# Adding loads of three units, later silu and closer first loads in a one-core decoder layer

## The chip, the core and the metric

The kernel runs on one core of one Trainium2 chip. The metric is the device time of one launch in microseconds, lower being better. One core has five engines with a queue of instructions each: TensorE (PE; PEld is its loading of weights), VectorE (DVE), ScalarE (ACT), GpSimd (POOL) and SyncE (SP). SP only issues transfers (DMA), and POOL issues some too. Each engine works through its queue in order, and an instruction that waits holds everything behind it on the same engine.

## The reference

A decoder layer over 256 tokens of width 2048 in float32, with three blocks, each added to the stream:

- `x + 1/2 * SwiGLU_1(rms(x))`, where `SwiGLU(h) = (silu(h @ w_gate) * (h @ w_up)) @ w_down` with an inner width of 5632,
- a mixer: one projection `h @ w_in` to q, k, v, u, v_sg and two gates; dilated causal attention in three groups beside a gated spatial mixing; both projected, weighted by sigmoid gates, summed and projected by `w_out`,
- `x + 1/2 * SwiGLU_2(rms(x))`, then a final RMS norm.

Nearly all of the work is products of 256 x K activations with weights that are read from memory (the page counts 466 MB read in all).

## The kernel before

**Products.** A float32 product is made of three products of rounded halves: the weights are split into `wh` (a rounded copy, made by ScalarE) and `wl = w - wh` (by VectorE), the activations into `xhi`, `xlo` likewise. A product of 512 columns over one weight tile of 128 x 512 is `xhi*wh + xhi*wl + xlo*wh` for each of the two blocks of 128 tokens.

**Steps and units.** An ordinary step takes two weight tiles (a raw unit of 512 KB, loaded by SP into one of four rooms, asked for four units ahead), has ScalarE and VectorE split them into a ring of nine places (`split`, lines 376 to 390), and issues 12 matmuls. This is one unit of the planner's time. `split` runs four steps ahead of the matmuls; a place of the ring is free when the matmuls of the step four back are done.

**Quads.** Two products that stand beside each other (gate and up, or two column blocks) share part of their K range by the seven-product scheme of Strassen and Winograd. Such a stretch is a quad. It has four blocks of weights, `b11`, `b21` (from the first product) and `b12`, `b22` (from the second), which the code numbers 0, 1, 2, 3, and `nq` units in each. Seven forms (p1 to p7) are split and multiplied in half-unit steps of 6 matmuls (for `nq` = 4: two steps of two units' tiles for each form). Three of the forms are sums that VectorE makes first: `f = b12 + b22`, `t2 = f - b11`, `t1 = t2 - b22` (written over `b11`), `t4 = b21 - t2`. t2 and t4 lie in the tile V. Forms of the activations are sums too (`sums_of`, lines 461 to 484: four small operations on VectorE, then a copy on ScalarE and a difference on VectorE).

In each product pair of the SwiGLU halves (`nq` = 4, 8 ordinary steps) the order is n p5 n p4 n p3 n p2, then p1 of the next quad, n n, p6 of the next, n, p7 of the next, n. So a quad's p1, p6, p7 come at the end of the pair before it, and its p5, p4, p3, p2 in its own pair. One pair takes 15 units.

**Rooms and loads of blocks.** All quads of a home (a SwiGLU half, or the mixer's `gates` and `merge`) use the same four rooms. `move_in` (line 308) asks for the blocks of a home's first quad at set waits. After that, `split` asks for a block of the next quad once the form that read the room last has been split: p5 frees block 0, p2 block 1, p7 block 2, p3 block 3 (`FREES`), 1 unit later for p5 and 2 units later for the others (line 390). Blocks are 1 MB at `nq` = 4.

**The adding load.** In the homes of the SwiGLU halves, all quads but the first let the DMA make f: after the load of block 2 (by SP), POOL issues loads of block 3's weights that add onto block 2's room (`accum_op`, lines 326 to 329), two units at a time: two loads of 512 KB at `nq` = 4, one of 512 KB and one of 256 KB at `nq` = 3, one of 512 KB at `nq` = 2. Block 3 itself is loaded too, for t1 and p3. 17 quads with adding loads have `nq` = 4 (8 in the first half, 9 in the second), four have 3, eight have 2.

**When the sums are made.** `prepare_ready` (line 347) runs after each step. It makes the next sum of a quad's list when its blocks were asked for 3 units ago, its forms are split and VectorE's metered load allows it; or, without those conditions, when the first step that needs it is within two steps of being split. At `nq` = 4 this second case holds for t2 in all 17 quads: it is emitted right behind the split of p1. A unit or more before it, SP was asked for block 3.

**Silu and hold.** When the up product of an inner block f closes, `post_up` runs `go` (silu of the gate on ScalarE), a unit later `mul` (VectorE), then a `turn` (`blocks`: VectorE transposes, SP writes 512 KB to memory; `back`, 3 units later: SP reads it in four loads of 128 KB; `ev`, 8 units later: the split into hA, hB). At some f the turned tile also gives sums for the down product's quads (f=0 and 1 in the first part of each half, f=4, f=8). Those still read the tile that the next silu writes. `holds["sg"]` keeps the next `post_up` back, a unit at a time, until `let_go`, which `sums` calls as `then()` right after its four operations.

**Extras.** `extra` puts VectorE work on a heap with a due time; `work_off` emits it when the metered load allows, at the latest when due.

Of the kernel before, what the change touches and what calls it, by code (L numbers as in the profile page):

```python
# [14 lines left out]
OP = mybir.AluOpType  # L15
# [33 lines left out]
FULL = 2.9  # L49
# [22 lines left out]
def layer(ctx: ExitStack, tc: tile.TileContext, a, out):  # L72
# [41 lines left out]
    x = big.tile([P, NT, D], F32, name="x")  # L114
# [33 lines left out]
    def lay_out():  # L148
        i, count = 0, 0
        while i < len(gemms):  # L150
            g = gemms[i]
            size, stage = g["group"]
            quad = g["quad"]
            taken = range(quad["k0"] // 2, quad["k0"] // 2 + quad["nq"]) if quad else ()
            order = [(p, q) for p in range(size) for q in range(gemms[i + p]["nk"] // 2) if q not in taken]
            if stage:
                order.sort(key=lambda s: stage(*s, gemms[i + s[0]]["nk"] // 2))
            new = [("n", (gemms[i + p], q // 2, q % 2)) for p, q in order]
            if quad:
                nq = quad["nq"]  # L160
                quad["gemms"] = gemms[i], gemms[i + 1]
                quad["loaded"], quad["split"] = {}, set()
                quad["adds"] = quad["home"] in homes and any(q["home"] is quad["home"] for q in quads)
                quad["todo"] = ["t2", "t1", "t4"] if quad["adds"] else ["f", "t2", "t1", "t4"]
                chunks = [(0, nq)] if nq < 4 else [(q, q + 2) for q in range(0, nq, 2)]
                for k, form in opening(count):
                    for c in chunks:
                        steps.insert(len(steps) - k, ("s", (quad, form, *c)))
                for k, form in reversed(list(closing(len(order)))):
                    for c in reversed(chunks):  # L170
                        new.insert(k, ("s", (quad, form, *c)))
                quads.append(quad)
                for h in quad["gemms"]:
                    h["left"] = [3 * (h["nk"] - nq)] * NT
                gemms[i + 1]["left"][1] += 9 * nq
            steps.extend(new)
            count = len(order) if size > 1 else 16
            i += size
        t, pos = -1.0, 0
        for kind, s in steps:  # L180
            width = 2 if kind == "n" else s[3] - s[2]
            t += 1 if kind == "n" else width / 4
            ends.append(t)
            slots.append([(pos + q) % RING for q in range(width)])
            pos += width
            if kind == "s":
                s[0].setdefault("at", {}).setdefault(s[1], len(ends) - 1)
            if kind == "n":
                hus.append(s)
                s[0]["steps"] += 1  # L190
            else:
                s[0]["gemms"][s[1] in ("p3", "p5", "p6", "p7", "p1")]["steps"] += 1
# [21 lines left out]
    def at(i, fn):  # L214
        heapq.heappush(callbacks, (i, next(counter), fn))

    now = [0.0, 0.0]
# [90 lines left out]
    def move_in(home):  # L308
        home["room"] = home["make"](home)
        first = next(q for q in quads if q["home"] is home)  # L310
        for b, wait in ((0, 0), (2, 1.5), (3, 3), (1, 5)):
            at(now[0] + wait, lambda b=b: load_block(first, b))

    def block(quad, b):
        g, j, nq = quad["gemms"][b // 2], b % 2, quad["nq"]
# [3 lines left out]
    def load_block(quad, b):  # L319
        if quad is None:  # L320
            return
        if not quad["loaded"]:
            started.append(quad)
        quad["loaded"][b] = now[0]
        SP.dma_start(blocks_of(quad)[b], block(quad, b))
        if b == 2 and quad["adds"]:
            for q in range(0, quad["nq"], 2):
                c = slice(q, min(q + 2, quad["nq"]))
                POOL.dma_start(blocks_of(quad)[b][:, c], block(quad, 3)[:, c], accum_op=OP.add)  # L329

    def blocks_of(quad):
        r = quad["home"]["room"]
        return [v[:, 0:quad["nq"]] for v in r[:-1]] + [r[-1]]

    def prepare(quad, what):
        b11, b21, b12, b22, t2, t1, _ = blocks_of(quad)
        out, x, y, op = {"f": (b12, b12, b22, OP.add), "t1": (t1, t2, b22, OP.subtract),
                         "t2": (t2, b12, b11, OP.subtract), "t4": (t2, b21, t2, OP.subtract)}[what]
        DVE.tensor_tensor(out, x, y, op=op)

# [6 lines left out]
    def prepare_ready():  # L347
        for quad in started:
            if not quad["todo"]:
                continue  # L350
            what = quad["todo"][0]
            blocks, forms = NEEDS[what]
            urgent = quad["at"]["p6" if what == "f" else next(f for f in USES if USES[f] == what)] - done <= 2
            if (all(quad["loaded"].get(b, 1e9) + (0 if urgent else 3) <= now[0] for b in blocks)
                    and quad["split"].issuperset(forms)
                    and (urgent or DVE.load + 0.56 * quad["nq"] <= FULL)):
                prepare_next(quad)

    def prepare_for(quad, form):
# [16 lines left out]
    def split(i, k=None):  # L376
        kind, s = steps[i]
        if kind == "s":
            quad, form, q0, q1 = s
            prepare_for(quad, form)  # L380
            if q1 == quad["nq"]:
                quad["split"].add(form)
        r = raws[place[i]] if kind == "n" else form_of(quad, form)[:, q0:q1]
        for first, end in runs(i, k or range(len(slots[i]))):
            o = slots[i][first]
            wh, wl = (v[:, o:o + end - first] for v in ring)
            ACT.activation(wh, r[:, first:end], AF.Copy)  # L387
            DVE.tensor_tensor(wl, r[:, first:end], wh.bitcast(F32), op=OP.subtract)
        if kind == "s" and form in FREES and q1 == quad["nq"]:
            at(now[0] + (1 if form == "p5" else 2), lambda: load_block(next_of(quad), FREES[form]))  # L390

    def product(g, t, act, w):
        g["left"][t] -= 1
# [67 lines left out]
    def sums_of(i, keep, q0, nq, store, v, name, tag="gate", slack=1, then=None):  # L461

        got = {}

        def sums():
            w = v[:, 0:4 * nq].rearrange("p (q m) i b -> p m q i b", m=4)
            a0, a1, b0, b1 = (w[:, m] for m in range(4))
            shape = [P, 4, nq, P]
            got["f"] = f = tmp(shape, f"fs{name}") if tag == "tmp" else sb.tile(shape, F32, tag=tag, bufs=2, name=f"fs{name}")
            s1, s2, s3, s4 = (f[:, k].rearrange("p q (i b) -> p q i b", b=32) for k in range(4))  # L470
            DVE.tensor_tensor(s1, a1, b1, op=OP.subtract)
            DVE.tensor_tensor(s2, a0, s1, op=OP.subtract)
            DVE.tensor_tensor(s3, a1, a0, op=OP.subtract)
            DVE.tensor_tensor(s4, b0, s2, op=OP.subtract)
            if then:
                then()
            at(now[0] + min(2, slack), parts)

        def parts():
            keep["both"] = both = store()  # L480
            split_psum(*both, got["f"], slack // 2)
            keep.setdefault("forms", {}).update({q0 + q: [v[:, :, q] for v in both] for q in range(nq)})

        at(i + 1, lambda: extra(0, slack, 0.6 + 0.6 * nq, sums) if slack > 1 else sums())
# [63 lines left out]
    xT = {}  # L548
# [58 lines left out]
    def turn_x(i, n, c, lag, read=3):  # L607
        def evac(src):
            for k in range(4 * c, 4 * c + 4):
                v, g = src[:, 2 * (k - 4 * c):2 * (k - 4 * c) + 2], gcols[:, 16 * n + k:16 * n + k + 1]  # L610
                ACT.activation(v, v, AF.Copy, scale=g)  # L611
            hi, lo = (turned(xT[p][:, 4 * c:4 * c + 4]) for p in ("hi", "lo"))
            split_psum(hi, lo, src, 1 if n and c < 3 else 0)
            tag = "tmp"
            if c == CS[n]:
                sums_of(i + lag, xT, 0, 2, forms_tile(big, "oT", f"fx{n}", 2), src, f"x{n}", tag)
            elif n != 1 and c == CS[n] + 1:
                def store():
                    return [big.tile([P, 4, 2, P], F32R, tag=tag, name=f"fy{n}{tag}") for tag in ("k2", "spare")]

                sums_of(i + lag, xT, 2, 2, store, src, f"y{n}", tag)

        turn(i, f"x{n}_{c}", 8, put_tokens(lambda: x[:, :, c * NC:(c + 1) * NC]),
             lambda: flat(sb.tile([P, NT, NC], F32, tag="gate", bufs=2, name=f"xt{n}_{c}")), evac, lag, read)
# [747 lines left out]
```

## Time and profile before

| | us |
|---|---|
| median of 3 runs | 2032.39 |
| lowest, highest | 2026.04, 2035.64 |
| the profiled execution | 2033.3 |
| its span, first to last instruction | 2031.6 |
| busy in the span: PE | 1981.2 |
| PEld | 1719.4 |
| DVE | 1660.8 |
| ACT | 1231.9 |
| POOL | 76.8 |
| mean granted clock of PE | 0.991 |

The time of an execution is the span plus 1.7 us around it. Busy times of different engines overlap. PE's matmuls are pipelined, and a busy PE is shown with modelled ends, so the number of matmuls in a stretch says more than its busy time. A line number in a row (L66, L329) is that of the kernel; L66 is the helper through which all VectorE operations go, so rows of VectorE are told apart by the tiles they write and read (`V<-quads` is t2, `quads<-V,quads` is t1, `wl<-raw,wh` is the split of an ordinary step). In a row `[7.04 <-DMA quads<-...]` the engine stood idle for 7.04 us before the instruction, and a transfer ended that. SPq and POOLq mark rows of the queues that issue transfers.

### The profile page before, as it was taken

How to read it: one execution, taken by the hardware profiler on the slowest of the kernel's cores; microseconds unless marked ns; L12 is line 12 of the kernel's file. 1: busy time of each engine (PE TensorE's matmuls, PEld its weight loads, DVE VectorE, ACT ScalarE, POOL GpSimd, SP SyncE). 2: the span in 40 equal slices, each digit the busy share in tenths (PEclk: the TensorE clock that was granted, in tenths of full speed). 3: DMA queues.
4: the chain of work that ended last, by engine and by line, in shares of the span. 5: the costliest groups of instructions: out<-in, count | busy, mean ns of one | idle time of the engine just before them, and what ended most of it. 6: DMA issues, size and time to landing. Idle time of an engine off the chain costs nothing.

```text
span 2031.6 us, 25234 instructions
## 1 busy us (share of the span) xinstructions
PE 1981.2 (98%) x9131; PEld 1719.4 (85%) x9131; DVE 1660.8 (82%) x1745; ACT 1231.9 (61%) x1472; POOL 76.8 (4%) x69
## 2 busy tenths in 40 slices
PE   9999999998999989999999999999999999999998
PEld 8788888887888878888888888888888888878887
DVE  6799898987998679676665777899998899888886
ACT  6466566665666566454554555676665566656664
POOL 0000010000000000000000000000000000000000
PEclk9999999999999999999999999999999999999999
DMA  9788878787877885888778667788779778877783
GB/s 302 264 253 243 282 223 274 240 269 210 268 223 230 257 298 171 245 277 267 256 236 256 207 208 227 233 261 273 249 244 272 229 238 252 252 223 245 231 269 134
DMA packets 266821, 497.32 MB, mean 245 GB/s; under 512 B 17228, under 2 KB 45768, under 8 KB 266568
## 3 DMA queue, kind: packets, MB, share of 16 engines
q1 hardware_dynamic: 253288, 470.01, 70.2%
q0 software_dynamic: 13088, 25.17, 7.4%
q8 instruction: 71, 1.16, 0.2%
q10 hardware_dynamic: 320, 0.53, 0.1%
q14 instruction: 54, 0.44, 0.1%
HBM read 465.99 MB, written 29.66 MB: 244 GB/s over the span
## 4 chain that ended last, share of the span: by engine, by line
PE 62%; DVE 8%; DMA 6%; issue 5%; ACT 1%; POOL 0%; SPq 0%; DVEq 0%; POOLq 0%; ACTq 0%
PE qd L394 43%; PE mm L394 18%; DVE wl L66 5%; DMA quads<-in_ffn_w_up_dram 3%; DMA raw<-in_w_in_dram 1%; ACT wh L387 1%; DMA quads<-in_w_in_dram 1%; DVE V L66 1%; DMA xt<-bmx 1%; DMA bmh529.0_10447<-bth529.0_10444 0%; DVE quads L66 0%; ACT xt L611 0%; POOL quads L329 0%; DVE xlo L66 0%; DVE btx L66 0%
## 5 line engine op out<-in xcount | busy, mean ns | idle before, releaser
L66 DVE TENSOR_TENSOR wl<-raw,wh 128x1024 fp32r<-128x1024 f32 (+1 forms) x593 | 647.0, 1110 | 205.1 <-ACT wh L387 202.7
L387 ACT ACTIVATE wh<-raw 128x1024 fp32r<-128x1024 f32 (+1 forms) x593 | 567.5, 966 | 362.2 <-PE qd L394 187.8
L387 ACT ACTIVATE wh<-quads 128x1024 fp32r<-128x1024 f32 (+2 forms) x315 | 308.3, 987 | 229.0 <-PE qd L394 206.5
L394 PE MATMUL qd<-wl,xhi 128*128 128x512 f32 x1106 | 420.9, 381 | 12.3 <-DVE wl L66 12.3
L394 PE MATMUL qd<-wh,xhi 128*128 128x512 f32 x1106 | 419.9, 380 | 1.9 <-ACT wh L387 1.9
L394 PE MATMUL qd<-wh,xlo 128*128 128x512 f32 x1106 | 419.3, 379 | 0.6 <-DVE xlo L66 0.6
L66 DVE TENSOR_TENSOR wl<-quads,wh 128x1024 fp32r<-128x1024 f32 (+2 forms) x315 | 349.7, 1136 | 76.6 <-ACT wh L387 74.8
L394 PEld LDWEIGHTS qd<-wl,xhi 128*128 128x128 f32 x1106 | 209.0, 189 | 47.7 <-DVE wl L66 18.4
L394 PE MATMUL mm<-wl,xhi 128*128 128x512 f32 x608 | 231.2, 383 | 7.8 <-DVE wl L66 7.8
L394 PEld LDWEIGHTS qd<-wh,xhi 128*128 128x128 f32 x1106 | 209.0, 189 | 33.9 <-ACT wh L387 4.2
L394 PE MATMUL mm<-wh,xlo 128*128 128x512 f32 x608 | 233.0, 383 | 1.7 <-DVE xlo L66 1.7
L394 PEld LDWEIGHTS qd<-wh,xlo 128*128 128x128 f32 x1106 | 209.0, 189 | 30.2 <-DVE xlo L66 1.0
L394 PE MATMUL mm<-wh,xhi 128*128 128x512 f32 x608 | 233.1, 383 | 0.0
L394 PE MATMUL qd<-wl,hA 128*128 128x512 f32 x564 | 217.0, 385 | 13.2 <-DVE wl L66 13.2
L394 PE MATMUL qd<-wh,hB 128*128 128x512 f32 x564 | 216.6, 384 | 0.0
L394 PE MATMUL qd<-wh,hA 128*128 128x512 f32 x564 | 216.3, 384 | 0.0
L387 ACT ACTIVATE wh<-V 128x1024 fp32r<-128x1024 f32 (+2 forms) x128 | 124.6, 995 | 93.0 <-PE qd L394 46.2
L66 DVE TENSOR_TENSOR wl<-V,wh 128x1024 fp32r<-128x1024 f32 (+2 forms) x128 | 143.0, 1141 | 16.1 <-ACT wh L387 15.2
L394 PEld LDWEIGHTS mm<-wl,xhi 128*128 128x128 f32 x608 | 116.1, 191 | 26.1 <-DVE wl L66 9.6
L394 PEld LDWEIGHTS qd<-wl,hA 128*128 128x128 f32 x564 | 108.3, 192 | 30.2 <-DVE wl L66 14.4
L394 PEld LDWEIGHTS mm<-wh,xlo 128*128 128x128 f32 x608 | 116.2, 191 | 19.0 <-DVE xlo L66 2.4
L394 PEld LDWEIGHTS mm<-wh,xhi 128*128 128x128 f32 x608 | 116.1, 191 | 16.9 <-ACT wh L387 0.4
(435 smaller groups left out, 2398.6 us busy)
## 6 DMA issues: line engine op xcount, KB each, us to landing
raw<-in_w_in_dram SPq DMA_DIRECT2D x168, 512.0 KB, 4.9
raw<-in_ffn_w_down_dram SPq DMA_DIRECT2D x120, 512.0 KB, 5.2
raw<-in_ffn_w_gate_dram SPq DMA_DIRECT2D x92, 512.0 KB, 4.2
raw<-in_ffn_w_up_dram SPq DMA_DIRECT2D x92, 512.0 KB, 5.8
quads<-in_ffn_w_gate_dram SPq DMA_DIRECT2D x38, 1024.0 KB, 7.9
quads<-in_ffn_w_up_dram SPq DMA_DIRECT2D x38, 1024.0 KB, 7.8
quads<-in_ffn_w_up_dram POOLq DMA_DIRECT2D x34, 512.0 KB, 8.1
quads<-in_ffn_w_down_dram SPq DMA_DIRECT2D x32, 512.0 KB, 5.2
```

The lines of the kernel that those rows point to most:

```text
L66: return method(out, *args, **kwargs)
L387: ACT.activation(wh, r[:, first:end], AF.Copy)
L394: PE.matmul(g["ps"][t], act, in_turn(w), start=not g["begun"][t], stop=g["left"][t] == 0, skip_group_check=g["quad"] is not None)
```

## The change

Four things are changed.

- The adding load takes up to three units in one DMA. At `nq` = 4 the fourth unit's f is made by VectorE (`f` on the slice from 3 to 4), which puts "f" ahead of t2 in those quads' lists, and with it the need for block 3.
- The load of block 2 (and with it the adding load) is asked for 1 unit after the split of p7 in place of 2.
- `let_go` after `sums` comes 2 units after the sums. The activation sums of the second column block before the second half (`y2`) become extra work with a slack of 3 units; until now they were made at once, one unit after the column block.
- `move_in` asks for the blocks 0, 2, 3, 1 at 0, 1, 2 and 3.5 units in the SwiGLU halves in place of 0, 1.5, 3 and 5, and all at once for `gates` and `merge`.

```diff
@@ lay_out
-                quad["todo"] = ["t2", "t1", "t4"] if quad["adds"] else ["f", "t2", "t1", "t4"]
+                quad["added"] = min(nq, 3) if quad["adds"] else 0
+                quad["todo"] = ["f"] * (quad["added"] < nq) + ["t2", "t1", "t4"]
@@ move_in
-        for b, wait in ((0, 0), (2, 1.5), (3, 3), (1, 5)):
-            at(now[0] + wait, lambda b=b: load_block(first, b))
+        late = home in homes
+        for b, wait in ((0, 0), (2, 1), (3, 2), (1, 3.5)):
+            at(now[0] + wait * late, lambda b=b: load_block(first, b))
@@ load_block
         if b == 2 and quad["adds"]:
-            for q in range(0, quad["nq"], 2):
-                c = slice(q, min(q + 2, quad["nq"]))
-                POOL.dma_start(blocks_of(quad)[b][:, c], block(quad, 3)[:, c], accum_op=OP.add)
+            c = slice(0, quad["added"])
+            POOL.dma_start(blocks_of(quad)[b][:, c], block(quad, 3)[:, c], accum_op=OP.add)
@@ prepare
-        out, x, y, op = {"f": (b12, b12, b22, OP.add), "t1": (t1, t2, b22, OP.subtract),
+        if what == "f":
+            c = slice(quad["added"], quad["nq"])
+            DVE.tensor_tensor(b12[:, c], b12[:, c], b22[:, c], op=OP.add)
+            return
+        out, x, y, op = {"t1": (t1, t2, b22, OP.subtract),
                          "t2": (t2, b12, b11, OP.subtract), "t4": (t2, b21, t2, OP.subtract)}[what]
@@ prepare_ready
-                    and (urgent or DVE.load + 0.56 * quad["nq"] <= FULL)):
+                    and (urgent or DVE.load + 0.56 * (quad["nq"] - (what == "f") * quad["added"]) <= FULL)):
@@ split
-            at(now[0] + (1 if form == "p5" else 2), lambda: load_block(next_of(quad), FREES[form]))
+            at(now[0] + (2 if form in ("p2", "p3") else 1), lambda: load_block(next_of(quad), FREES[form]))
@@ sums_of, sums
             if then:
-                then()
+                at(now[0] + 2, then)
@@ turn_x
-                sums_of(i + lag, xT, 2, 2, store, src, f"y{n}", tag)
+                sums_of(i + lag, xT, 2, 2, store, src, f"y{n}", tag, slack=3 if n else 1)
```

## The prediction

> **What bounds the kernel now.** I read the page first, then TensorE's gaps one by one, then the windows around them, then the DMA queues behind those windows.
>
> ```profile
> PE 1981.2 (98%) x9131; PEld 1719.4 (85%) x9131; DVE 1660.8 (82%) x1745; ACT 1231.9 (61%) x1472; POOL 76.8 (4%) x69
> ```
>
> TensorE bounds the kernel, and nothing in the change touches a matmul. So only time that TensorE loses can move. The windows view of the stretches where it loses most (columns: width, busy us and instructions of PE, PEld, DVE, ACT, POOL, then granted clock, DMA share, GB/s):
>
> ```profile
> 240.00:280.00 40.00, 40.00 (x187) 35.03 (x186) 37.38 (x35) 24.27 (x27) 8.48 (x6) 1.00 0.79 245
> 465.00:480.00 15.00, 9.47 (x33) 7.63 (x32) 8.23 (x8) 5.02 (x6) 0.00 (x0) 0.79 0.65 187
> 1575.00:1590.00 15.00, 11.95 (x48) 9.86 (x47) 10.64 (x9) 6.92 (x8) 0.00 (x0) 0.89 0.55 170
> 1800.00:1815.00 15.00, 10.36 (x37) 8.31 (x36) 8.86 (x10) 5.42 (x7) 0.00 (x0) 0.78 0.67 199
> 325.00:332.00 7.00, 5.96 (x28) 4.89 (x28) 6.22 (x5) 4.68 (x6) 0.00 (x0) 1.00 1.05 379
> 1845.00:1855.00 10.00, 8.20 (x38) 6.86 (x38) 6.60 (x7) 5.37 (x7) 0.00 (x0) 1.00 0.73 210
> 1888.00:1895.00 7.00, 6.25 (x30) 5.15 (x29) 5.39 (x5) 4.73 (x6) 0.00 (x0) 1.00 1.06 345
> 348.00:358.00 10.00, 8.16 (x36) 6.28 (x35) 7.72 (x11) 9.05 (x11) 2.31 (x2) 1.00 0.90 226
> 1913.00:1923.00 10.00, 8.20 (x36) 6.32 (x35) 8.62 (x11) 8.18 (x10) 0.00 (x0) 1.00 0.62 162
> 78.00:98.00 20.00, 16.43 (x61) 13.27 (x60) 18.65 (x18) 8.95 (x11) 0.00 (x0) 0.83 0.54 168
> 715.00:735.00 20.00, 14.77 (x56) 11.89 (x55) 15.01 (x15) 11.16 (x16) 0.00 (x0) 0.83 0.75 260
> 1350.00:1356.00 6.00, 3.81 (x18) 2.69 (x16) 6.00 (x7) 5.97 (x10) 0.00 (x0) 1.00 0.62 183
> ```
>
> The first row is a full stretch: 187 matmuls in 40 us, 0.214 us each, so a unit (12 matmuls) is 2.57 us. Where the clock stayed at 1.00, the loss is width minus PE busy. Where it fell, I count missing matmuls instead: 15 us hold 70, so the rows at 465, 1575 and 1800 miss 37, 22 and 33, or 7.9, 4.7 and 7.1 us.
>
> **The change part by part. First the adding load.** The first six short windows (465 to 1888) have one cause. t2 (V<-quads on VectorE) waits for the second adding load, and that one is issued only when the first has landed:
>
> ```profile
> L66 DVE TENSOR_TENSOR V<-quads 128x2048 f32<-128x2048 f32 (+2 forms) x36 | 66.3, 1842 | 25.5 <-DMA quads<-in_ffn_w_up_dram 21.8 <-issue 3.6
> ```
> ```profile
> 453.64 1.22 POOL L329 DMA_DIRECT2D quads<-in_ffn_w_up_dram  x1 [31.61 <-DVE hB L66]
> 462.18 1.21 POOL L329 DMA_DIRECT2D quads<-in_ffn_w_up_dram  x1 [7.32 <-issue]
> ```
> ```profile
> 463.51 1.23 DVE L66 TENSOR_TENSOR wl<-quads,wh 128x1024 fp32r<-128x1024 f32 x1 [0.72 <-ACT wh L387]
> 471.77 2.29 DVE L66 TENSOR_TENSOR V<-quads 128x2048 f32<-128x2048 f32 x1 [7.04 <-DMA quads<-in_ffn_w_up_dram]
> ```
> ```profile
> quads<-in_ffn_w_up_dram POOLq DMA_DIRECT2D x34, 512.0 KB, 8.1
> ```
> ```profile
> quads<-in_ffn_w_down_dram POOLq DMA_DIRECT2D x4, 256.0 KB, 11.7
> ```
>
> Two halves in a row take 8.1 + 8.1 = 16.2 us. In the four quads of three units the 512 KB and 256 KB loads go out together, and the later half lands 11.7 us after its issue; I take 12 us for one load of 768 KB. That is 4 us sooner, and the raw block's load moves one step ahead (half a unit, 1.3 us; it passes at most one raw load of 512 KB, asked for four units ahead). The six waits of VectorE behind the TensorE losses are 1.6 to 7.0 us. 5.3 us clears all but at most 1.7 us of the longest, about the cover that is worked out below. Taken off: 7.9 + 4.7 + 7.1 + 1.04 + 1.80 + 0.75 = **23.3 us**. At the low end (one load of 768 KB as slow as two halves) only 1.3 us at each of six, 7.8 us.
>
> **What the fourth unit costs.** The 17 quads of four units outside the first get an f of 128x512 on VectorE ahead of t2:
>
> ```profile
> L66 DVE TENSOR_TENSOR V<-V,qd 128x512 f32<-128x512 f32 x36 | 24.5, 679 | 0.0
> ```
>
> That is 0.68 us each, 11.5 us in all, and no bound by itself: VectorE is idle 2.6 of 40 us in the full stretch above. What matters is the wait that f brings. It reads block 3, of which until now only t1 had need, some three units later. By the planner's due times f stands where t2 stood, and block 3 is asked for 0.5 to 1.5 units ahead of it. Behind a waiting f on VectorE stand the wl of the next unit, t2, and the wl after it. How long may f wait?
>
> ```profile
> 512.53 2.29 DVE L66 TENSOR_TENSOR V<-quads 128x2048 f32<-128x2048 f32 x1
> 514.73 1.22 DVE L66 TENSOR_TENSOR wl<-raw,wh 128x1024 fp32r<-128x1024 f32 x1
> ```
> ```profile
> 516.79 0.38 PE L394 MATMUL qd<-wl,xhi 128*128 128x512 f32 x1
> ```
>
> Now the next wl ends at 515.95 and is used at 516.79: 0.8 us of cover. With the new order (f 0.68, wl 1.14, t2 2.20, wl 1.22, from 512.53) the second wl ends at 517.8 and is used a unit later, at 519.4: 1.6 us of cover. So TensorE loses what f waits beyond 1.6 us. The first and the last of the 17 quads, in the order asked, landed after so many us, t2:
>
> ```profile
> 122.06 0.49 SPq L325 DMA_DIRECT2D quads<-in_ffn_w_up_dram  x1
> ```
> ```profile
> quads<-in_ffn_w_up_dram SPq DMA_DIRECT2D x1, 1024.0 KB, 6.6
> ```
> ```profile
> 127.28 2.28 DVE L66 TENSOR_TENSOR V<-quads 128x2048 f32<-128x2048 f32 x1
> ```
> ```profile
> 1881.51 2.31 SPq L519 DMA_DIRECT2D sg680.5_13320<-bmh687.5_13361  x4
> 1883.92 0.85 SPq L283 DMA_DIRECT2D raw<-in_ffn_w_up_dram  x1
> 1884.81 0.74 SPq L325 DMA_DIRECT2D quads<-in_ffn_w_up_dram  x1
> ```
> ```profile
> quads<-in_ffn_w_up_dram SPq DMA_DIRECT2D x1, 1024.0 KB, 9.8
> ```
> ```profile
> 1880.73 1.21 POOL L329 DMA_DIRECT2D quads<-in_ffn_w_up_dram  x1 [7.10 <-DVE wl L66]
> ```
> ```profile
> 1889.65 2.29 DVE L66 TENSOR_TENSOR V<-quads 128x2048 f32<-128x2048 f32 x1 [1.61 <-DMA quads<-in_ffn_w_up_dram]
> ```
>
> In the first, block 3 lands at 128.7 against t2's 127.3: f would wait 1.4 us. In the last it lands at 1894.6, and t2 could have begun at 1888.0: 6.6 us. Here SyncE stood at the read-back of the turned h (L519) until 1881.5, and the second adding load shared the DMA engines. All 17 worked out this way wait 59 us, 35 of it beyond 1.6. But the second adding load goes away, and alone block 3 took 6.6 us. With 6.9 us, a little over that, nine quads whose block 3 is asked for without a read-back ahead wait under 1.6 us; three more join them since the silu edit moves their read-back behind block 3. The other five (f=4 and 8 of both halves, f=0 of the second) wait 4.2, 3.1, 3.4, 3.1 and 3.7 us: 17.5 - 5 x 1.6 = 9.5 us lost. I add 3.5 for landings that scatter: **+13 us**, between 0 and 35.
>
> **Silu two steps back.** At five places like the windows at 348 and 1913 (the first and the last of five) ScalarE stands in a silu whose tile VectorE is still reading for sums:
>
> ```profile
> 348.37 1.27 ACT L655 ACTIVATE sg117.5_2540<-qd,rstd 128x512 f32<-128x512 f32 x2 [5.17 <-DVE fsh109.5_2523 L66]
> ```
>
> TensorE loses 1.8 us in each of the two windows, some 8 us over the five. The sums are emitted at their last due time there, so two steps later means that the whole tail of that f (silu, product, two transposes, a write of 512 KB and four reads of 128 KB on SP's queue) comes one unit later, while ScalarE goes on with the wh that wait behind it. New cost: the sums' copy and the silu now stand together on ScalarE (2.3 us), and in the first half the shift passes on from f=1 to f=3, whose h the down product needs at once. I take **-6 us**; bounds -8 and 0.
>
> **The openings.** Each first quad asks for its blocks closer together: in the windows at 78 and 715 TensorE loses 32 and 37 matmuls, 7.0 and 8.0 us.
>
> ```profile
> 73.60 1.22 DVE L66 TENSOR_TENSOR wl<-raw,wh 128x1024 fp32r<-128x1024 f32 x1 [2.65 <-ACT wh L387]
> 74.75 2.28 DVE L66 TENSOR_TENSOR quads<-quads 128x2048 f32<-128x2048 f32 x1
> ```
> ```profile
> 720.21 1.22 DVE L66 TENSOR_TENSOR quads<-quads 128x1024 f32<-128x1024 f32 x1 [4.92 <-DMA quads<-in_w_in_dram]
> ```
>
> At 74.75 the first f comes a unit sooner, into the 2.65 us in which VectorE stood idle: -3 us (0 to -7). At 720, block 3 passes three raw loads and one of 768 KB on SP's queue and lands some 3 us sooner, but those raw loads then go behind 1.5 MB more and hold the next wh: -1.5 us (+5 to -5). In the third opening block 1 goes ahead of the read-back of x (its due time, 3.5 after the start, precedes that of the read-back):
>
> ```profile
> 1366.23 2.84 SPq L519 DMA_DIRECT2D xt<-bmx  x4
> 1369.34 0.39 SPq L283 DMA_DIRECT2D raw<-in_ffn_w_gate_dram  x1
> 1370.84 0.39 SPq L325 DMA_DIRECT2D quads<-in_ffn_w_gate_dram  x1
> ```
>
> 1 MB more ahead at the 260 GB/s of the row at 715 is 4 us; I take it that what follows the read-back has no cover: +4 us (0 to +6). The y2 sums with slack 3 leave the crowded stretch at 1350 (2.2 us lost): -2 us (+2 to -2). Together **-2.5 us**. The four loads of merge come at once too: 0, since none of the losing windows lies there, or +2 if raw loads fall behind.
>
> **Sum:** -23.3 + 13 - 6 - 2.5 = -18.8 us. The profiled execution took 2033.3 us (0.9 above the median, so no correction): 2033.3 - 18.8 = **2014.5 us**.
>
> **The rivals.** (1) *Block 3 becomes the wait.* If its landings stay as they are, f loses 35 us instead of 13, and seven of the 17 losses are 3.0 us or longer, where the clock falls: the windows at 465, 1575 and 1800 lost 2 to 3 us beyond their idle time. At 2 us each that is 14 more: 2033.3 - 23.3 + 49 - 8.5 = 2050, slower. It decides once the 17 waits beyond 1.6 us exceed 32 us with their clock. For it: the last quad above; against it: the load that shared its time goes. The Trainium skill (TensorE: Matmul & The Clock Gate, Part 1: The HAM clock gate) has the clock fall only after an idle window of about 3.4 us; the window at 1575 fell to 0.89 after a shorter gap (12.0 busy of 15), so the row is used. By the page four of the seven would pay: 2044. (2) *One load of 768 KB lands as late as two.* Then t2 keeps waiting: -7.8, f waits beside it (+9.5 at the five quads), silu -6, openings -2.5: about 2026. For it: 11.7 us for 256 KB beside 512 KB; against it: that is still under 16.2. (3) *The gains are given back at the openings:* the bursts push raw loads, +5 at the mixer, +6 in the third, +2 for y2 and nothing at the first, and silu brings 0: 2033.3 - 23.3 + 13 + 13 = 2036, or with silu's 6 about 2030. (4) *Block 3 never decides* and all windows close: 2033.3 - 23.3 - 8 - 7 = 1995.
>
> **How the numbers follow.** Forecast 0.48 (its own range 2004 to 2023), rival 1 0.13, rival 2 0.09, rival 3 0.17, rival 4 0.13. Some 0.5% (10 us) is what a measurement of this kernel can tell from no change: faster is below 2022, slower above 2042.5. Faster: nearly all of the forecast, rival 4, a little of 2: 0.62. Slower: rival 1 and a corner of 3: 0.14. Same: 0.24. The range of 1996 to 2042 leaves out rival 1 and the far half of rival 4.
>
> **What would show it.** One POOL row per quad at the adding line, none released by the one before; t2's idle time on the adding load near 0 (now 21.8); a new row of VectorE, quads<-quads 128x512 x17, with idle time on quads<-in_ffn_w_up_dram: under 20 us by the forecast, 59 by rival 1. Silu without the 5 us idle rows. The windows at 465, 1575 and 1800 back at clock 1.00. Wrong would be a t2 or f that still waits over 3 us in more than two quads, or raw loads late after 720 and 1370.

## The result and the profile after

The changed kernel takes **2044.74 us** (median of 4 runs, 2043.85 to 2048.88) beside 2030.26 us for the kernel before on the same chip. The ratio is **1.0074, 95% interval 1.0044 to 1.0103**: about 15 us slower, where 18.8 us faster was forecast. The profiled execution took 2048.88 us, its span is 2047.2.

The page after, engines and the adding loads (last figure: median us from issue to landing):

```profile
PE 1981.4 (97%) x9131; PEld 1711.0 (84%) x9131; DVE 1670.7 (82%) x1762; ACT 1226.1 (60%) x1472; POOL 53.7 (3%) x48
...
quads<-in_ffn_w_up_dram POOLq DMA_DIRECT2D x17, 768.0 KB, 9.6
```

TensorE's work is the same, 9131 matmuls. VectorE has 17 instructions and 10 us more. The load of 768 KB lands 9.6 us after its issue (12 was taken). The groups of instructions by shape, after; the first is t2, the second f:

```profile
L66 DVE TENSOR_TENSOR V<-quads 128x2048 f32<-128x2048 f32 x19 | 43.4, 2284 | 0.0
...
L66 DVE TENSOR_TENSOR quads<-quads 128x512 f32<-128x512 f32 x17 | 11.7, 690 | 35.0 <-DMA quads<-in_ffn_w_up_dram 31.7 <-DMA gcols<-gm 3.4
```

t2's 21.8 us of idle time on the adding load are gone. f's wait has come in its place: VectorE stands idle 35.0 us ahead of the 17 f. What TensorE waited for, before and then after (total us, times, longest):

```profile
PE qd L394 <- DVE wl L66: 27.2, 22, 5.5
...
PE qd L394 <- DVE V L66: 1.7, 2, 1.6
```
```profile
PE qd L399 <- DVE wl L66: 28.3, 40, 2.6
PE qd L399 <- DVE V L66: 10.2, 11, 1.7
PE qd L399 <- DVE hB L66: 6.2, 2, 3.5
```

The waits for wl are about as long in total as before, in 40 pieces instead of 22. The waits for V have grown from 1.7 to 10.2 us. This V is not t4: it is `V<-V,qd`, with which VectorE empties a bank of results so that TensorE may write it again. A new kind is the wait for hB, the low half of an h form. The windows view after (columns as in the prediction):

```profile
370.00:380.00 10.00, 7.44 (x34) 5.86 (x33) 5.93 (x6) 3.06 (x4) 0.00 (x0) 1.00 0.92 282
...
1470.00:1480.00 10.00, 7.50 (x35) 5.92 (x33) 5.99 (x5) 3.12 (x4) 0.00 (x0) 1.00 0.97 309
1592.00:1607.00 15.00, 15.00 (x71) 13.12 (x71) 14.17 (x13) 9.38 (x11) 0.00 (x0) 1.00 0.54 179
1817.00:1832.00 15.00, 15.00 (x70) 12.82 (x70) 11.15 (x11) 8.03 (x10) 0.00 (x0) 1.00 0.78 274
...
203.00:213.00 10.00, 7.22 (x33) 5.70 (x32) 9.02 (x9) 5.58 (x6) 0.00 (x0) 1.00 0.98 347
```

The long losses that stood at 1575 and 1800 are closed, with the clock at 1.00 (the same matmuls run 17 us later in the changed kernel, hence these windows). New losses of 2.5 us stand at 370 and 1470 (f) and of 2.8 us at 203 (hB). At 370, SyncE's queue, VectorE and TensorE in the order of time (start, us, what; idle time before it and what ended that):

```profile
366.62 0.46 SPq L327 DMA_DIRECT2D quads<-in_ffn_w_up_dram  x1
```
```profile
369.50 1.21 DVE L66 TENSOR_TENSOR wl<-quads,wh 128x1024 fp32r<-128x1024 f32 x1
374.71 0.69 DVE L66 TENSOR_TENSOR quads<-quads 128x512 f32<-128x512 f32 x1 [4.00 <-DMA quads<-in_ffn_w_up_dram]
375.32 1.22 DVE L66 TENSOR_TENSOR wl<-raw,wh 128x1024 fp32r<-128x1024 f32 x1
```
```profile
374.13 0.38 PE L399 MATMUL qd<-wh,xhi 128*128 128x512 f32 x1
376.59 0.48 PE L399 MATMUL qd<-wl,xhi 128*128 128x512 f32 x1 [2.08 <-DVE wl L66]
```

Block 3 is asked for at 366.62 and lands 8.1 us later. VectorE is ready for f at 370.71 and stands until 374.71; the wl behind f ends at 376.54, and TensorE has waited 2.08 us for it. This is the mechanism that the prediction named and priced at 13 us. The question is what else costs.

### The profile page after: what moved, and what is told of

Same layout as the page of the kernel before. It is cut to its first block, busy times and chain, and to the rows that moved or that the text cites. A ratio compares the mean times of both kernels' runs of the same rounds, so it can differ in the third digit from the quotient of the medians.

```text
span 2047.2 us, 25218 instructions
## 1 busy us (share of the span) xinstructions
PE 1981.4 (97%) x9131; PEld 1711.0 (84%) x9131; DVE 1670.7 (82%) x1762; ACT 1226.1 (60%) x1472; POOL 53.7 (3%) x48
## 4 chain that ended last, share of the span: by engine, by line
PE 62%; DVE 17%; DMA 10%; issue 5%; ACT 3%; SPq 1%; POOL 0%; DVEq 0%; ACTq 0%; POOLq 0%
PE qd L399 44%; PE mm L399 18%; DVE wl L66 10%; DMA quads<-in_ffn_w_up_dram 3%; DVE V L66 3%; ACT wh L392 2%; DMA raw<-in_w_in_dram 1%; DMA xt<-bmx 1%; DMA raw<-in_ffn_w_gate_dram 1%; DVE quads L66 1%; DVE hB L66 1%; SPq L524 1%; DMA more<-in_ffn_w_gate_dram 0%; DVE x L66 0%; DMA raw<-in_ffn_w_down_dram 0%
## 5 line engine op out<-in xcount | busy, mean ns | idle before, releaser
L66 DVE TENSOR_TENSOR wl<-V,wh 128x1024 fp32r<-128x1024 f32 (+2 forms) x128 | 142.6, 1142 | 27.9 <-ACT wh L392 26.0
L399 PE MATMUL qd<-wh,fx 128*128 128x512 f32 x352 | 120.7, 384 | 10.6 <-DVE V L66 10.2
```

Of the source, the lines that this page charges most:

```text
L66: return method(out, *args, **kwargs)
L399: PE.matmul(g["ps"][t], act, in_turn(w), start=not g["begun"][t], stop=g["left"][t] == 0, skip_group_check=g["quad"] is not None)
```

## The experiments

All ratios are to the kernel before, with 95% intervals. The expectations count a planner's unit as 3.5 us; it is 2.57 us (12 matmuls of 0.214), so a step moved by a unit was expected to do more than it can. Where they speak of V as t4, it is the bank's `V<-V,qd`.

My first theory after the result blamed the silu line, because the new small gaps lie behind the sums. Four kernels took the change apart.

**Silu at once, the rest as changed.**

```diff
             if then:
-                at(now[0] + 2, then)
+                then()
```

> The changed kernel with one line put back: silu follows the four sums in the same unit, as in the kernel before. Theory A (standing silu back is what costs; the adding loads themselves gain): the changed kernel's TensorE gaps sum to 84.6 us against 67.4 before; the adding loads' wait (21.8 us) is gone, VectorE's f costs 12.3 us in its place, the openings come to about -1, so some 27 us of gaps have another origin, and A puts them on the silu line: 2044.7 - 27 = 2018 us, 0.993 to 0.995 of the kernel before. Theory B (VectorE's f, which now waits for block 3, costs the time): silu made a gain of about 6 us, so undoing it gives 2044.7 to 2051 us, 1.007 to 1.010. Theory C (the closer openings cost it): no change, 2045 us.

Measured: 2047.64 us, ratio 1.0091 (1.0077 to 1.0105). Undoing the line gains nothing; its interval overlaps that of the change itself.

**The silu line alone, in the kernel before.**

```diff
             if then:
-                then()
+                at(now[0] + 2, then)
```

> The kernel before with the silu line alone: silu two units after the sums. Theory A: 2030 + 22 to 27 = 2052 to 2057 us, a ratio of 1.011 to 1.013, with stalls of the last h form (hB) of each half and small TensorE gaps behind the sums. Theory B and C: the forecast's -6 to 0, 2024 to 2030 us, 0.997 to 1.000.

Measured: 2033.73 us, 1.0011 (0.9998 to 1.0025): nothing either way. TensorE's groups by operand show why a line that does what it says gives nothing, in this kernel and then in the kernel before:

```profile
L394 PE MATMUL qd<-wh,xhi 128*128 128x512 f32 x1106 | 419.4, 379 | 0.2 <-ACT wh L387 0.2
...
L394 PE MATMUL qd<-wh,hB 128*128 128x512 f32 x564 | 217.0, 385 | 5.2 <-DVE hB L66 5.2
...
L394 PE MATMUL qd<-wl,fx 128*128 128x512 f32 x176 | 67.2, 382 | 6.1 <-DVE wl L66 6.1
```
```profile
L394 PE MATMUL qd<-wh,xhi 128*128 128x512 f32 x1106 | 419.9, 380 | 1.9 <-ACT wh L387 1.9
...
L394 PE MATMUL qd<-wh,hB 128*128 128x512 f32 x564 | 216.6, 384 | 0.0
...
L394 PE MATMUL qd<-wl,fx 128*128 128x512 f32 x176 | 67.1, 381 | 0.6 <-DVE wl L66 0.6
```

The waits for ScalarE's wh at silu go (1.9 to 0.2 us), but 5.5 us appear at fx, a few steps later, and 5.2 us at hB. TensorE's waits for wl in all fall from 27.2 to 23.6 us, the 5.5 at fx included, so the other waits for wl fell by some 9 us and the whole comes out near nothing.

**The adding part alone** (one load of three units, f of the fourth on VectorE, block 2 a unit sooner): the change without its silu line, `move_in` and `slack=3` lines.

> The kernel before with the adding part alone: one adding load of three units, VectorE's f for the fourth, block 2 loaded a unit sooner; silu and the openings as before. Theory A: 2030 - 21.8 (t2's wait) + 12.3 (f's wait) - 3 (clock no longer held back after the long gaps) = 2018 us, 0.993 to 0.995. Theory B: the whole loss is here, 2044 to 2050 us, 1.007 to 1.010. Theory C: faster as in A or a little more.

Measured: 2055.38 us, 1.0125 (1.0110 to 1.0140): 25 us slower. Theory A has fallen: the whole loss is here, and more.

**The openings alone** (`move_in` and the y2 slack).

> The kernel before with the openings alone: first blocks closer together and the last y sums with three units of slack. Theory A and B: first opening -1.8, mixer -1.7, third opening +2.8, y about 0 or -2: 2027 to 2031 us, 0.998 to 1.000. Theory C: 2042 us or more, 1.006 and above.

Measured: 2022.87 us, **0.9968** (0.9957 to 0.9978). They gain 6.5 us. The windows of this kernel:

```profile
78.00:98.00 20.00, 17.34 (x81) 14.87 (x80) 20.00 (x18) 10.06 (x13) 0.00 (x0) 1.00 0.59 179
715.00:735.00 20.00, 18.53 (x86) 15.93 (x85) 18.98 (x20) 15.83 (x20) 0.00 (x0) 1.00 0.84 305
1350.00:1356.00 6.00, 4.68 (x22) 3.82 (x21) 6.00 (x8) 4.68 (x9) 0.00 (x0) 1.00 0.71 246
...
1362.00:1386.00 24.00, 19.80 (x82) 16.14 (x81) 17.71 (x14) 12.19 (x17) 0.00 (x0) 0.93 0.72 229
```

Against 61, 56 and 18 matmuls in the first three before, these hold 81, 86 and 22: 4.3, 6.4 and 0.9 us gained. The last stretch held 106 before:

```profile
1362.00:1386.00 24.00, 23.03 (x106) 19.72 (x105) 20.32 (x20) 14.32 (x20) 1.06 (x1) 1.00 0.94 313
```

It loses 24 matmuls, 5.1 us. Together -6.5 us, as measured. The match is closer than the traces warrant: the two profiled executions differ by 4.7 us (2028.6 and 2033.3), and this kernel reaches the later stretches up to 8 us sooner, so they don't hold the same work to the matmul.

The next four took the adding part apart.

**Block 2 a unit sooner, alone**, with two adding loads and no f:

```diff
-            at(now[0] + (1 if form == "p5" else 2), lambda: load_block(next_of(quad), FREES[form]))
+            at(now[0] + (1 if form in ("p5", "p7") else 2), lambda: load_block(next_of(quad), FREES[form]))
```

> The kernel before with block 2 of the next quad (and the adding loads behind it) a unit sooner, alone: still two adding loads of two units, no f on VectorE. The adding part alone came out at 2055.4 us, 25 us over before, so the question is which piece of it. Theory B1 (VectorE's f stands in order and waits for block 3) and B2 (f is one more step in the chain f, t2, t1, t4, so t4 comes a unit late): this piece is harmless, and each of the six waits of t2 shrinks by one unit of 3.5 us: TensorE's gaps 1.04, 5.5, 3.05, 4.6, 1.8 and 0.75 leave about 2 and 1: 2030.6 - 14 = 2017 us, 0.992 to 0.995. Theory B3 (the sooner load itself does harm: t2 and t1 of the three-unit quads come ahead of hB on VectorE, and the transfers collide): 2035 us or more, above 1.002.

Measured: 2024.68 us, 0.9966 (0.9953 to 0.9979): harmless, with half the gain expected. t2 still waits 13.7 us, now in two places. GpSimd's queue in this kernel shows that at the window near 470 the sooner start bought nothing (the second load started at 462.18 before):

```profile
450.67 1.22 POOL L329 DMA_DIRECT2D quads<-in_ffn_w_up_dram  x1 [30.36 <-DMA quads<-in_ffn_w_up_dram]
462.38 1.21 POOL L329 DMA_DIRECT2D quads<-in_ffn_w_up_dram  x1 [10.48 <-issue]
```

**Block 3 a unit sooner, in the adding part:**

```diff
-            at(now[0] + (2 if form in ("p2", "p3") else 1), lambda: load_block(next_of(quad), FREES[form]))
+            at(now[0] + (2 if form == "p2" else 1), lambda: load_block(next_of(quad), FREES[form]))
```

> The adding part alone (2055.4 us) with block 3 loaded one unit after p3's split, not two, so that it lands some 3.5 us sooner for VectorE's f. The waits of f were 0.4 to 3.3 us there, so nearly all of them end. Theory B1: with the wait go the 12 us of TensorE's gaps right behind f and the small gaps that trail it (V, fy0k, xhi, some 16 us): 2027 us, 0.995 to 1.000 of before. Theory B2: only the 12 us go, the trailing gaps stay: 2043 us, 1.005 to 1.007. Theory B3: no change or worse, 1.012.

Measured: 2030.47 us, 0.9997 (0.9984 to 1.0010): 25 us less than the adding part, from the time of one load. f and TensorE's waits in the adding part, and then here:

```profile
L66 DVE TENSOR_TENSOR quads<-quads 128x512 f32<-128x512 f32 x17 | 11.8, 691 | 36.6 <-DMA quads<-in_ffn_w_up_dram 36.6
```
```profile
PE qd L398 <- DVE wl L66: 27.9, 38, 2.3
PE qd L398 <- DVE V L66: 9.9, 11, 1.6
```
```profile
L66 DVE TENSOR_TENSOR quads<-quads 128x512 f32<-128x512 f32 x17 | 11.7, 685 | 5.7 <-DMA quads<-in_ffn_w_up_dram 5.7
```
```profile
PE qd L398 <- DVE wl L66: 10.0, 15, 1.0
PE qd L398 <- DVE V L66: 9.0, 11, 1.6
```

f's wait is nearly gone, TensorE's waits for wl are at 10.0 us, and yet the kernel is only even with the one before. Going by the distances of its matmuls (worked out as in the table below, without those at half clock), TensorE lost 18.1 us within 6.5 us of the starts of the 17 f in the adding part and 0.5 us here, and between 6.5 and 18 us behind them 8.3 and 1.3 us. The waits for V stay, so they are not the wait's doing.

**f in t2's unit** (three steps in the list; f issued right ahead of t2):

```diff
-                quad["todo"] = ["f"] * (quad["added"] < nq) + ["t2", "t1", "t4"]
+                quad["todo"] = ["f"] * (quad["added"] == 0) + ["t2", "t1", "t4"]
...
+        if what == "t2" and 0 < quad["added"] < quad["nq"]:
+            prepare(quad, "f")
```

> The adding part alone with f issued in the same unit as t2, right ahead of it, so that the chain has three steps as before; the waits for block 3 stay at the same instruction. Theory B1: the same or a little more than 2055 us, 1.011 to 1.014, since VectorE waits as before. Theory B2: t4 comes a unit sooner, TensorE's waits for V (8.3 us in ten places, 0.7 to 1.0 us each) end: 2047 us or less, 1.006 to 1.009.

Measured: 2053.68 us, 1.0108 (1.0086 to 1.0129). Each theory got half. TensorE's waits:

```profile
PE qd L402 <- DVE wl L66: 36.6, 26, 4.2
...
PE qd L402 <- DVE V L66: 1.6, 1, 1.6
```

The waits for V are back at 1.6 us with the fourth step gone, as B2 said. TensorE's waits for wl, now with less time between f and p6, grew by as much (27.9 to 36.6 us), although f itself idles less (28.9 us). TensorE's mean granted clock is 0.987 here against 0.995 in the adding part, so part of the loss is time at half clock.

**f on GpSimd:**

```diff
-            DVE.tensor_tensor(b12[:, c], b12[:, c], b22[:, c], op=OP.add)
+            (POOL if quad["added"] else DVE).tensor_tensor(b12[:, c], b12[:, c], b22[:, c], op=OP.add)
```

> The adding part alone with f of the fourth unit as a GpSimd instruction in place of a VectorE one; its place in the chain is kept. VectorE's splits then no longer stand behind f's wait; t2 follows a unit of 3.5 us later and waits only for what is left. Theory B1: the 12 us behind f and the 16 us trailing it go: 2027 us, 0.995 to 1.001. Theory B2: the trailing gaps stay, 2043 us, 1.005 to 1.007. If GpSimd's instruction is itself slow (several us), t2 waits for it: 2055 or more.

Measured: 2050.21 us, 1.0091 (1.0065 to 1.0117). The wait only changes its place, to t2:

```profile
L66 DVE TENSOR_TENSOR V<-quads 128x2048 f32<-128x2048 f32 x19 | 43.5, 2289 | 30.4 <-POOL quads L339 26.0 <-DMA quads<-in_ffn_w_gate_dram 4.3
...
L339 POOL TENSOR_TENSOR quads<-quads 128x512 f32<-128x512 f32 x17 | 23.3, 1370 | 345.6 <-DMA quads<-in_ffn_w_up_dram 345.6
```

GpSimd takes 1.37 us for what VectorE does in 0.69, and t2, which stands on VectorE ahead of the same splits, waits 26.0 us for it.

Then came mends, and the old cause by itself.

**The change with block 3 a unit sooner** (the edit shown above).

> The changed kernel with one number altered: block 3 is loaded one unit after p3's split, not two. Theory B1 (VectorE's f waits for block 3, and all of VectorE stands behind it) as the adding part alone showed it (block 3 sooner took it from 2055.4 to 2030.5): 2044.7 - 25 = 2020 us, 0.993 to 0.996 of before. Rival (the openings and silu line have their own late block, which block 3 sooner pushes back further): 2035 us or more, above 1.002.

Measured: 2029.11 us, 0.9998 (0.9986 to 1.0011). One number takes 15 us away, which is the loss, and not the 25 us that it took from the adding part: the openings' 6.5 us do not show on top. f waits 11.7 us here and hB 7.5 us, against 5.7 and 4.4 without openings and silu line.

**Both mends on the adding part** (f in t2's unit, block 3 a unit sooner).

> The adding part alone with both: f in the same unit as t2 (three steps in the chain, as before) and block 3 a unit sooner. With block 3 sooner alone the time was 2030.5 us, and TensorE still waited 0.7 to 0.9 us for V in ten places (about 8 us). Theory B1 with B2 (the wait and the longer chain are two costs): 2022 us, 0.994 to 0.998. Theory B1 alone (the V gaps are another form of the same wait): no gain over 2030 us, since f's wait a unit before p6 has less cover.

Measured: 2023.17 us, 0.9967 (0.9956 to 0.9978). Step and wait are two costs: with both mended the adding part gains.

**Openings and the sooner block 2.**

> The kernel before with the openings (0.9968) and with block 2 a unit sooner (0.9966), and two adding loads as before. If the two are separate: 2031 - 7.7 - 6.5 = 2016 us, 0.992 to 0.995. If the sooner block 2 collides with the closer first blocks: 2022 us, no more than either alone, 0.996 to 0.998.

Measured: 2020.12 us, 0.9958 (0.9940 to 0.9975). Separate gains would give 0.9934, just below the interval, but each of the two gains has an interval of its own, so it isn't shown whether part of them is shared.

**A larger ring for GpSimd's descriptors**, the kernel before otherwise:

```diff
-    nc = _bacc.Bacc("TRN2", target_bir_lowering=False, num_devices=1, dynamic_dma_scratch_size=1024)
+    nc = _bacc.Bacc("TRN2", target_bir_lowering=False, num_devices=1, dynamic_dma_scratch_size=1280)
```

> The kernel before with more room for GpSimd's DMA descriptors (1280 bytes in place of 1024), nothing else: both adding loads of two units can be in flight together, where the second of them was issued only when the first had landed (8 to 12 us later). Theory: the second lands some 3.4 us sooner (one load of 768 KB landed 9.8 us after its issue, so 1 MB in two should take about 13, not 16.2), TensorE's gaps behind t2 of 1.04, 5.5, 3.05, 4.6, 1.8 and 0.75 us leave 3.3: 2031 - 13 = 2017 us, 0.992 to 0.995. Rival (the transfers share the same bandwidth with the blocks on SyncE's queue, so nothing lands sooner): 2031 us, 0.998 to 1.001.

Measured: 2007.87 us, **0.9896** (0.9881 to 0.9911). GpSimd's queue and the groups in this kernel:

```profile
450.34 2.48 POOL L329 DMA_DIRECT2D quads<-in_ffn_w_up_dram  x2 [31.30 <-DVE wl L66]
```
```profile
L66 DVE TENSOR_TENSOR V<-quads 128x2048 f32<-128x2048 f32 x19 | 43.4, 2285 | 1.4 <-DMA quads<-in_ffn_w_up_dram 1.4
```

Both loads go out back to back, and t2's waits fall from 21.8 to 1.4 us. What kept the second load back was room for its descriptors; 256 bytes more do what the change wanted, with no f and no new wait. It gains 21 us, where 13 were expected.

The last runs had to price f's step apart from its wait.

**Block 3 a unit later, in the adding part** (`{"p2": 2, "p3": 3}.get(form, 1)` in the same line).

> The adding part alone with block 3 three units after p3's split, a unit of 3.5 us later than in the change; the number of steps and the work are the same. Theory B1 (the wait sets the price): f's idle time grows from 36.6 us by up to 17 x 3.5 = 60; a us of it cost 25/31 = 0.8 us when it went from 36.6 to 5.7, so 2055 + 40 to 50 = 2095 to 2105 us, 1.031 to 1.037. Theory B2 (the step, not the wait): 2055 to 2070 us, below 1.020.

Measured: 2055.67 us, 1.0130 (1.0109 to 1.0152), no more than the adding part. It decides nothing: f idles 38.5 us against 36.6, and in 14 of the 17 quads SyncE's queue has the same order in the trace as in the adding part, so there the edit moved nothing. Block 3's load starts 6.5 us ahead of f in both (f at 330 and at 327 us).

**A fourth step that waits for nothing**, beside the larger ring:

```diff
-                quad["todo"] = ["t2", "t1", "t4"] if quad["adds"] else ["f", "t2", "t1", "t4"]
+                quad["todo"] = ["f"] * (nq == 4) + ["t2", "t1", "t4"] if quad["adds"] else ["f", "t2", "t1", "t4"]
...
+        if what == "f" and quad["adds"]:
+            DVE.tensor_tensor(t2[:, 3:4], b11[:, 3:4], b11[:, 3:4], op=OP.add)
+            return
```

> The kernel before with the larger ring (2007.9 us) and one step more in each of the 17 quads of four units: an add of 128x512 on VectorE into a quarter of t2's tile, which t2 then writes over; it reads block 0 alone and waits for no block 3. Theory B2 (f's step shifts t2, t1 and t4 by a unit, and t4 comes too late for TensorE): 2008 + 7 to 10 = 2016 us, 0.992 to 0.995, with waits for V of 0.7 to 0.9 us. Theory B1 alone (only a wait costs; 17 x 0.69 us of VectorE's time lie under TensorE): 2008 to 2010 us, 0.989 to 0.991.

Measured: 2025.47 us, 0.9979 (0.9967 to 0.9991), 17 us over the larger ring alone. The add never waited, and the waits of the changed kernel are back:

```profile
L66 DVE TENSOR_TENSOR V<-quads 128x512 f32<-128x512 f32 x17 | 11.6, 684 | 0.0
...
PE qd L397 <- DVE V L66: 7.2, 9, 1.6
PE qd L397 <- ACT wh L390: 5.1, 7, 0.9
PE qd L397 <- DVE hB L66: 2.6, 1, 2.6
```

One of them, VectorE and then TensorE:

```profile
386.28 2.29 DVE L66 TENSOR_TENSOR V<-quads,V 128x2048 f32<-128x2048 f32 x1
388.49 2.35 DVE L66 TENSOR_TENSOR wl<-quads,wh 128x1024 fp32r<-128x1024 f32 x2
390.76 0.68 DVE L66 TENSOR_TENSOR V<-V,qd 128x512 f32<-128x512 f32 x1
```
```profile
391.49 0.48 PE L397 MATMUL qd<-wh,fx 128*128 128x512 f32 x1 [0.78 <-DVE V L66]
```

The bank's `V<-V,qd` stands behind t4 and two wl without a pause, so what comes late there stays late. The lateness begins one step back, in ScalarE's queue and then VectorE's:

```profile
372.72 2.10 ACT L390 ACTIVATE wh<-V 128x1024 fp32r<-128x1024 f32 x3 [2.28 <-DVE V L66]
```
```profile
377.26 1.23 DVE L66 TENSOR_TENSOR wl<-raw,wh 128x1024 fp32r<-128x1024 f32 x1 [1.02 <-ACT wh L390]
```

With the add as a step of its own, a wl stands between it and t2, so t2 starts a step later. ScalarE, which splits t2 for p6, idles 2.28 us for it, and VectorE then idles 1.02 us for ScalarE. With the larger ring alone VectorE goes on there with a pause of 0.05 us.

**The same add in t2's unit:**

```diff
+        if what == "t2" and quad["adds"] and quad["nq"] == 4:
+            DVE.tensor_tensor(t2[:, 3:4], b11[:, 3:4], b11[:, 3:4], op=OP.add)
```

> The kernel before with the larger ring (2007.9 us) and the same idle add of 128x512 in each of the 17 quads of four units, now issued right ahead of t2 in t2's own unit. Theory B2 (a step of its own is what costs): the 17.6 us go but for what 0.69 us more ahead of t2 costs: 2008 to 2012 us, 0.989 to 0.991. Rival (VectorE's 11.7 us of work cost as such, wherever they stand): 2020 us or more, above 0.995.

Measured: 2015.74 us, 0.9924 (0.9905 to 0.9942): between the two. By the medians, some 6 of the 17 us are the added work ahead of t2 (0.9896 to 0.9924) and some 11 its place as a step of its own (0.9924 to 0.9979). The intervals of the first two overlap slightly, and by the traces (table below) the two parts are about equal, so the split is rough.

**Larger ring and openings.**

> The kernel before with the larger ring (2007.9 us alone, 0.9896) and the openings (0.9968 alone). If the two are separate, as their places are (the six windows of t2 here, the first quads of each part there): 2008 - 7 = 2001 us, 0.985 to 0.988. If the openings' gain came out of the same waits of t2, nothing is added: 2008 us, 0.989 to 0.991.

Measured: 2001.81 us, **0.9865** (0.9843 to 0.9886). The gains are separate.

**Both mends and the openings.**

> The adding part with f in t2's unit and block 3 a unit sooner (0.9967 together), and the openings (0.9968 alone). If separate: 2016 us, 0.992 to 0.995. If the openings bring block 3 late again in the first quads, as it seems they did beside the changed kernel with block 3 sooner (0.9998, no better than without them): 2023 us, 0.996 to 0.998.

Measured: 2018.25 us, 0.9940 (0.9919 to 0.9960): the openings add 5.5 us here too.

**Larger ring, openings and block 2 sooner.**

> The larger ring and the openings (2001.8 us, 0.9865) with block 2 a unit sooner as well. Alone beside two loads in turn it gave 0.9966, out of t2's waits; with the larger ring those are 1.1 us in all, so nothing is left to gain: 2000 to 2003 us, 0.985 to 0.988. Rival (the sooner transfers collide with the raw loads): 2008 us or more, above 0.989.

Measured: 2000.37 us, **0.9845** (0.9824 to 0.9866): with no wait of t2 left, the sooner block adds nothing that can be told from the run before. These two beat both kernels; they are 27 and 31 us faster than the kernel before.

The runs stand together in one table. Lost time is worked out from each trace: for neighbouring matmuls in the stretches of the halves' quads (95 to 645 and 1397 to 1950 us), what the distance of their starts exceeds 0.216 us by, where that is over 0.1.

| kernel | ratio | lost in the halves' quads, us |
|---|---|---|
| before | 1 | 41.7 |
| changed | 1.0074 | 61.4 |
| adding part alone | 1.0125 | 65.7 |
| same, block 3 sooner | 0.9997 | 41.8 |
| same, f in t2's unit too | 0.9967 | 30.5 |
| larger ring | 0.9896 | 16.2 |
| larger ring, fourth step that waits for nothing | 0.9979 | 34.1 |
| larger ring, the same add in t2's unit | 0.9924 | 25.3 |

## Why the prediction was wrong

- **The adding load: right in size.** t2's idle time on it is 0.0, the loads go out one for a quad, and the clock is back at 1.00 in the windows near 1575 and 1800. The term was -23.3 us. The larger ring, which takes the same waits away and adds nothing, gained 21 us. (The low end of 7.8 us counted 1.3 us at windows that lose 1.04 and 0.75; it should have been 7.0.)
- **What the fourth unit costs: the step that failed.** It stood at +13 (0 to 35). Its rule, that TensorE loses what each f waits beyond 1.6 us, held: the 17 waits of the changed kernel (35.0 us in all, where the forecast had under 20 and rival 1 had 59) come to 15.4 us by it, and TensorE lost 17 us within 6.5 us of f. That 13 was near is in part luck, since eleven quads wait over 1.6 us and none over 4, where five were named at 3.1 to 4.2. What failed is that the term ended there. *The lateness behind:* the 1.6 us of cover were worked out for the first two wl behind f and for nothing later. Another 6 us are lost between 6.5 and 18 us behind f in the changed kernel, and block 3 a unit sooner took away 25 us in the adding part and 15 in the changed kernel. *The step:* f was called no bound by itself, since VectorE is idle 2.6 us of 40 in a full stretch. An add of the same size that waits for nothing cost 17 us, for its work and for its place, which puts t2 a step later. The average idle time of a stretch does not say whether there is any ahead of a bank's `V<-V,qd`; ahead of the one at 390 there was none for 13 us. Together, wait and step come to some 42 us by the runs of the parts. By difference it is 25 + 21 = 46 in the adding part and 15 + 21 + 6.5 - 2 = 40.5 in the changed kernel, if removing t2's waits is worth the larger ring's 21. The forecast had 13.
- **Silu two steps back: wrong.** -6 was taken, bounds -8 and 0; alone it measured +2.2 (-0.4 to +5.1). Its waits did shrink. The term named what would pay, f=3's h, "which the down product needs at once", and then gave it no price: 5.2 us at hB (one wait in each half, where the term named the first half) and 5.5 at fx, which it did not name. Taken out of the changed kernel, the line made no difference that can be told (1.0091 against 1.0074).
- **The openings: right in sign by place, too small at the mixer.** First -4.3 (forecast -3), third +5.1 (+4), y2 -0.9 (-2), and the mixer -6.4 instead of -1.5. The terms were worked out from idle time and landings alone, and in both places TensorE's clock stayed at 1.00 where it had been 0.83. At the mixer 3.8 of the 6.4 us are idle time (5.2 to 1.5) and the rest is the clock; at the first opening only 0.9 of the 4.3 is (3.6 to 2.7), so that term was near by luck. Together -6.5 instead of -2.5.
- **The sum by the runs:** -21 (waits of t2) + 25 (f's wait) + 17 (f's step) - 6.5 (openings) + 2 (silu) = +16.5 us; measured +15. The 25 are those of the adding part; with the 15 that a sooner block 3 took from the changed kernel itself the sum is 6.5, so its closeness proves little. The adding part's own three terms give +21 against 25 measured, so some 4 us of it have no name, and the openings' gain beside silu and a sooner block 3 is another 6 us that was not traced.
- **Rival 1** had the time nearly right (2050) and block 3 as the cause, but not the mechanism: it needed falls of the clock after seven waits of 3 us. (The losses beyond idle time that it went by, "2 to 3 us", are 2.4, 1.6 and 2.5 by its rows.) The changed kernel shows one at an f, the first, where TensorE waited 2.62 us until 127.6:

```profile
126.00:131.00 5.00, 3.36 (x9) 2.74 (x10) 4.93 (x5) 1.10 (x2) 0.00 (x0) 0.66 1.08 300
```

The loss came mostly from many small gaps and from work that waited for nothing.

## What to carry to other kernels

An instruction put into the queue of an engine that is nearly full costs its wait, the lateness of all that follows it until the queue next has a pause, its own work, and the delay of whatever it pushes a step back; look for the pause, not for the mean idle time. When a second transfer starts just as the first lands, ask first what it lacks: here 256 bytes of descriptor room were worth 21 us, and the way round them cost some 40. An edit that moves a wait is priced at the next place that has no slack, and that place belongs in the sum once it has been named.

## What was unexpected in the hardware

TensorE's clock fell after shorter pauses than I had counted on, and not after each. The windows view of the kernel with f in t2's unit, where TensorE stood idle for 2.30 us from 568, and then of the adding part alone, where it did for 2.96 us from 82:

```profile
570.00:573.00 3.00, 2.46 (x7) 2.03 (x8) 3.00 (x4) 3.00 (x5) 0.00 (x0) 0.68 0.43 109
573.00:577.00 4.00, 4.00 (x16) 3.33 (x16) 3.98 (x3) 1.67 (x2) 0.00 (x0) 0.81 0.68 207
```
```profile
81.00:90.00 9.00, 6.04 (x29) 4.96 (x28) 9.00 (x9) 4.69 (x6) 0.00 (x0) 1.00 0.58 191
```

A pause of 2.30 us was followed by half the clock for some 3.4 us (matmuls 0.43 us apart from 571.1 to 574.5), one of 2.96 us was not. Nor does the length alone decide: the same wait for hB, 2.63 us near 209, is followed by matmuls 0.41 to 0.43 us apart from 210.4 to 213.8 in the kernel with the silu line alone, and by none in the changed kernel (clock 1.00 in its row from 203). The Trainium skill (TensorE: Matmul & The Clock Gate, Part 1: The HAM clock gate) has the clock fall after an idle window of about 3.4 us and come back after a busy one of that length, with a window that runs free of the work. The length of the fall agrees; that a pause must be 3.4 us long does not.

An adding load of 768 KB took 9.6 us in the changed kernel (the median of 17). The Trainium skill (DMA: Bandwidth & Descriptors, Anatomy of one DMA — SWDGE (gpsimd) path) fits a transfer that GpSimd issues by 2.0 us plus its bytes over 436e3 per us, from which I estimate 3.8 us. The two aren't the same case, since these loads add and run beside SyncE's; the rows show only that the fit can't price them here.
